# Seven block products in a decoder layer's q/k and gate/v projections, overlapped attention heads, and no spill of the residual

## The chip, the cores and the metric

The kernel runs on one core of a Trainium2 chip. A core has a matrix engine (TensorE, PE in the profile, with its weight loads as PEld), three engines for elementwise work (VectorE or DVE, ScalarE or ACT, GpSimd or POOL), a queue engine (SyncE or SP) and 16 DMA engines that move data between memory and the core's own SBUF. TensorE writes into PSUM, of which this kernel uses eight banks. The metric is the device time of one execution in microseconds.

## The reference

Two decoder layers run over one residual stream h of 256 tokens by 2048 features, all in float32. Layer 0 has one input projection that feeds two groups of heads: sliding-window attention (16 query heads in 4 groups, each group with one key and value head) and an mLSTM with 4 heads of width 256. Layer 1 has forgetting attention (FoX, 16 heads of width 128). Each mixer is followed by a SwiGLU FFN.

```python
def swa_mlstm_mixer(xn, w_in, w_out, sinks, b_i, b_f, head_gain):
    proj = xn @ w_in
    q_s, k_s, v_s, q_m, k_m, v_m, o_m, i_m, f_m = split_cols(proj, EVEN_SIZES)
    attn = sliding_window_attention(q_s, k_s, v_s, sinks)        # heads reshaped
    i_pre = softcap(i_m + b_i)
    f_pre = softcap(f_m + b_f)
    h = mlstm_chunkwise(q_m, k_m, v_m, i_pre, f_pre)              # heads reshaped
    h = rms_norm(h, head_gain)
    mem = sigmoid(o_m) * h
    return concatenate([attn, mem]) @ w_out

def forgetting_attention_mixer(xn, w_in, b_f, w_out):
    q, k, v, f = split_cols(xn @ w_in, FOX_SIZES)
    c = cumsum(log_sigmoid(f + b_f))
    s = q @ k.T * scale + c[:, None] - c[None, :]                 # causal, softmax
    return (softmax(s) @ v) @ w_out

for layer in range(2):
    h = h + mixer(rms_norm(h, norm_mix[layer]))
    h = h + (silu(xn @ w_gate) * (xn @ w_up)) @ w_down            # xn = rms_norm(h, norm_ffn)
return rms_norm(h, norm_final)
```

## The kernel before

**How a product is made.** Every weight block of two k-tiles by 512 columns (512 KB) is loaded by SP into a raw tile, and split into a rounded part hi (ScalarE, L166) and a rest lo (VectorE, L167), both in the matrix engine's fast float32 form. The activations are split in the same way (xh, xl for the normed input; mh, ml for a mixer's or FFN's inner values). A product of a 128x128 activation block with a 128x512 weight block is then three matmuls (hi·xh, lo·xh, hi·xl), accumulated in one PSUM bank. There are two 128-row blocks of tokens, so an output of 512 columns takes two banks and 16 k-tiles x 2 row blocks x 3 = 96 matmuls: this is `project` with `gemm` (L182 to L199).

**Pairs with seven block products.** `pair_group` (L423) works two outputs of 512 columns at once, over the same activations. Its `order` lists eight positions of two k-tiles. A position marked 0 is plain: eight block products. A position marked 1 is mixed: sums and differences of the activation blocks (`sums_of`, L238, tile sx) and of the weight blocks (L462 to L465, VectorE) are formed, split again, and multiplied in seven block products, four of which go into banks of their own (prods). When the group ends, `prods` are combined (L490 to L494) and the four plain banks are added. The plain banks come from one PSUM pool and the prods from the other: pa (tag acc) and pm have four banks each, and a group whose plain banks lie in pa takes all of pm for its prods. The FFN and layer 1's q with k are made this way already; layer 0's mixer is not.

**Layer 0's mixer.** The order in the program is: k and v of SWA while x is transposed; the first half of SWA's q and its groups 0 and 1, the second half and groups 2 and 3 (`swa`, `attention` with its inner `rest`), each group brought to its end before the next begins; the last part of the output gate with the mLSTM gates' columns (264 columns) and the gate arithmetic (pu, pn, pb); the rest of the gate (512 and 256 columns); mLSTM's q, its k, the first half of v, heads 0 and 1, the second half of v, heads 2 and 3 (`mlstm`, L831); then the output projection `out_proj` (L400). The latter takes 12 of 16 k-tiles for two outputs first and the last four after them, so that head 3 (k-tiles 14 and 15) is wanted last. h is x all the while.

**Layer 1's mixer.** The last 256 columns of v with the forget gate (272 columns), the fourth v block (256), three sums of x, then for each of four head groups: q with k as a pair group, the previous attention's `rest`, the decay tile, that group's v, and the attention's first half. The split halves of mixed weights (hw) lie in the space of h, which was therefore written to memory (spill) at the end of layer 0 and is read back before layer 1's FFN.

**What sets the order.** Each engine runs its own instruction list in order. The lists are made ahead of time by a planner that goes through the program with a cost model: an instruction is placed when the planner thinks that its operands and its tile's slot are there, and later work that is ready is placed ahead of earlier work that is not. Tiles of one tag share a fixed number of slots (bufs): 6 for hi and lo, 4 for raw, 2 for hv, one for c. Some work has due positions (`later`, `todo`, run at a numbered step of a gemm or a group by `run_due`).

Of the kernel before, what the change touches and what calls it, by code (L numbers as in the profile page):

```python
# [43 lines left out]
MIX = ((0, 0), (1, 1), (0, 2), (1, 3), (0, 4), (1, 5), (0, 6), (0, 7))  # L44
NX = 3
# [14 lines left out]
def trunk(  # L60
# [43 lines left out]
    gn = [gp.tile([2 * KT, P], F32, name=f"gn{i}") for i in range(2)]  # L104
    nc.scalar.dma_start(gn[0], norm_mix.rearrange("l (k p) -> (l k) p", p=P))

    def load_raw(w, k0, c0, n, pool=wr, bufs=4):
        raw = pool.tile([P, CK, NB], F32, tag="raw", name="raw", bufs=bufs)
# [7 lines left out]
    spill = dp.tile([P, NT, D], F32, name="spill")  # L116
# [21 lines left out]
    nc.gpsimd.dma_start(gn[1], norm_ffn.rearrange("l (k p) -> (l k) p", p=P))  # L138
# [8 lines left out]
    gT = cp.tile([P, 4 * KT], F32, name="gT")  # L147

    def gain_columns(i):
        pg = pm.tile([P, NB], F32, tag="pm", name="pg")  # L150
        nc.tensor.transpose(pg[:, 0 : 2 * KT], gn[i], ident[0 : 2 * KT, 0 : 2 * KT])
        nc.vector.tensor_copy(gT[:, 2 * i * KT : 2 * (i + 1) * KT], pg[:, 0 : 2 * KT])
# [85 lines left out]
    def sums_of(pool, sh, sl, copies, full=None, tags=("tmp", "tmp")):  # L238
        if full is None:
            full = pool.tile([P, 2, NT, P], F32, tag=tags[0], name="full")  # L240
            copies(full.rearrange("p i t q -> p i (t q)"))
        s = pool.tile([P, 4, P], F32, tag=tags[1], name="s4")
# [6 lines left out]
    def split_scaled(idx, n, extra=None, joined=None):  # L249
        for half in range(2):  # L250
# [8 lines left out]
            for i in range(2):  # L259
                k = 4 * n + 2 * half + i  # L260
                src = pt[:, i, :, :].rearrange("p t q -> p (t q)")
                g = gT[:, idx * KT + k : idx * KT + k + 1]
                nc.scalar.mul(xh[:, k, :], src, g)
                nc.vector.scalar_tensor_tensor(
                    out=xl[:, k, :], in0=src, scalar=g, in1=xh[:, k, :].bitcast(F32), op0=ALU.mult, op1=ALU.subtract
                )
# [42 lines left out]

    def add_out(acc, n):  # L310
# [11 lines left out]
    def attention(sp, q_of, k_of, v_of, dv, scale, bias0, bias1, k_tile, sinks=None, negc=None, s_bufs=2):  # L322
        s = sp.tile([P, 4, 3 * P], F32, tag="s", name="s", bufs=s_bufs)
        for b, cols, bias in ((0, P, bias0), (1, S, bias1)):
# [3 lines left out]
            for half in range(2):  # L328
# [7 lines left out]
                    op1=ALU.add,  # L336
                )
# [61 lines left out]

    def out_proj(w, idx, key, extra):  # L400
# [22 lines left out]
    def pair_group(fp, par, lhs, sums, mats, order, todo=(), halves=None):  # L423
# [4 lines left out]
        t0, t1 = slice(0, P), slice(P, 2 * P)  # L428
        for pos, (kind, pair) in enumerate(order):
            k0 = 2 * pair  # L430
            if not kind:
# [18 lines left out]
            ra, rb = (load_raw(w, k0, c0, NB, fp, W_RAWS if halves else RAWS) for w, c0 in mats)  # L450
# [38 lines left out]
        c = fp.tile([P, 4, NB], F32, tag="c", name="c", bufs=1)  # L489
        nc.scalar.copy(c[:, 0, :], prods[0])  # L490
        nc.vector.tensor_tensor(out=c[:, 2, :], in0=prods[3], in1=c[:, 0, :], op=ALU.add)
        nc.vector.tensor_tensor(out=c[:, 1, :], in0=prods[2], in1=c[:, 2, :], op=ALU.add)
        nc.vector.tensor_tensor(out=c[:, 3, :], in0=prods[1], in1=c[:, 1, :], op=ALU.add)
        nc.vector.tensor_tensor(out=c[:, 2, :], in0=prods[1], in1=c[:, 2, :], op=ALU.add)  # L494
        return plain, c

    def ffn(layer, fp, sx, sd, key, todo, idx_next=None, key_next=None, finish=None):
# [6 lines left out]
        for g0, g1 in zip(PARTS, PARTS[1:]):  # L504
# [69 lines left out]
            def close(acc, n):  # L574
# [4 lines left out]
                else:  # L579
# [6 lines left out]
                    nc.gpsimd.dma_start(spill[:, :, n * NB : (n + 1) * NB], h[:, :, n * NB : (n + 1) * NB])  # L586
# [43 lines left out]
    with tc.tile_pool(name="ev", bufs=1) as ev:  # L630
        dist = ev.tile([P, S], F32, name="dist")
# [12 lines left out]
        gain = ev.tile([P, ML_H * VD], F32, name="gain")  # L644
        nc.gpsimd.dma_start(gain, mlstm_head_gain[0].partition_broadcast(P))

        def natural(sp, acc, n, name, scale=r):
# [442 lines left out]
```

## Time and profile before

| what | value |
|---|---|
| median of 3 runs (lowest, highest) | 2106.33 us (2106.03, 2108.21) |
| profiled execution | 2108.73 us |
| its span, first to last instruction | 2107.0 us |
| granted TensorE clock, mean | 0.998 |
| instructions | 26956 |
| DMA moved, mean rate | 430.92 MB, 205 GB/s |
| read from memory, written | 406.57 MB, 4.21 MB |

The profiled execution is a run of its own; its time is not among the three. Times in the rows are microseconds from the start of the span. A row of a group of instructions has busy time, the mean duration of one in nanoseconds, and the idle time of the engine just before them with what ended it. In rows of the timeline the idle time and its cause stand in brackets at the end. The row of busy time over the span in 40 slices shows how even the load is:

```profile
PE   8999999999999999999999999999999999999998
DVE  6675558999999999999887768679999999999994
ACT  6565458765577655767667665588655667556763
```

The first six slices (up to about 310 us) are layer 0's mixer, slices 20 to 26 (about 1040 to 1370 us) layer 1's; the others are FFNs and output projections.

### The profile page before, as it was taken

To read this page: it belongs to the slowest core of one execution; us is meant where nothing else is said; L and a number is where in the kernel's file an instruction comes from. 1 tells how busy PE (TensorE), PEld (TensorE's weight loads), DVE (VectorE), ACT (ScalarE), POOL (GpSimd) and SP (SyncE) were. 2 spreads that over 40 slices of the span, in tenths; PEclk is the share of its full clock that TensorE was granted. 3 is DMA by queue.
4 is the path that set the end of the run, shared out by engine and by line. 5 is a ranking of instruction groups with operands and counts; after the bars stand their busy time and mean duration, and the time that the engine had idled before them with its cause. 6 is when DMAs were issued, how large, how long until landed. Compare 5 with 4: busy or idle time off the path is not lost.

```text
span 2107.0 us, 26956 instructions
## 1 busy us (share of the span) xinstructions
PE 2089.5 (99%) x9583; PEld 1733.8 (82%) x9583; DVE 1783.3 (85%) x2322; ACT 1328.5 (63%) x1681; POOL 49.1 (2%) x75
## 2 busy tenths in 40 slices
PE   8999999999999999999999999999999999999998
PEld 7888888888888888888888888888888888888886
DVE  6675558999999999999887768679999999999994
ACT  6565458765577655767667665588655667556763
POOL 2010000000000000000000000000000000000000
PEclk9999999999999999999999999999999999999999
DMA  8454548666567666667587676486756567666663
GB/s 266 149 157 150 170 146 276 229 203 215 192 198 231 230 193 210 212 218 218 178 256 206 192 218 210 140 250 213 233 188 224 196 205 238 212 198 203 224 199 136
DMA packets 290855, 430.92 MB, mean 205 GB/s; under 512 B 89024, under 2 KB 97312, under 8 KB 290464
## 3 DMA queue, kind: packets, MB, share of 16 engines
q1 hardware_dynamic: 288896, 421.27, 63.2%
q0 software_dynamic: 1776, 7.92, 1.1%
q8 instruction: 75, 1.23, 0.2%
q14 instruction: 60, 0.49, 0.1%
q10 hardware_dynamic: 48, 0.02, 0.0%
HBM read 406.57 MB, written 4.21 MB: 195 GB/s over the span
## 4 chain that ended last, share of the span: by engine, by line
PE 98%; DMA 1%; ACT 0%; issue 0%; DVE 0%; POOLq 0%; POOL 0%; DVEq 0%; ACTq 0%
PE acc L416 19%; PE acc L418 19%; PE acc L417 19%; PE acc L197 8%; PE acc L199 8%; PE acc L198 8%; PE prod L418 5%; PE prod L416 5%; PE prod L417 5%; PE p L327 1%; PE po L386 1%; DMA raw<-in_w_in_odd_dram 1%; PE ptm L319 0%; PE pp L378 0%; PE po L387 0%
## 5 line engine op out<-in xcount | busy, mean ns | idle before, releaser
L166 ACT CAST hi<-raw 128x1024 fp32r<-128x1024 f32 (+2 forms) x669 | 679.9, 1031 | 517.4 <-PE acc L418 271.9
L167 DVE TENSOR_TENSOR lo<-raw,hi 128x1024 fp32r<-128x1024 f32 (+2 forms) x669 | 791.6, 1198 | 202.9 <-ACT hi L166 200.1
L417 PE MATMUL acc<-lo,xh 128*128 128x512 f32 x1118 | 435.1, 389 | 0.0
L416 PE MATMUL acc<-hi,xh 128*128 128x512 f32 x1118 | 434.9, 390 | 0.0
L418 PE MATMUL acc<-hi,xl 128*128 128x512 f32 x1118 | 431.8, 389 | 0.0
L418 PEld LDWEIGHTS acc<-hi,xl 128*128 128x128 f32 x1118 | 209.9, 188 | 44.2
L417 PEld LDWEIGHTS acc<-lo,xh 128*128 128x128 f32 x1118 | 209.8, 188 | 44.0
L416 PEld LDWEIGHTS acc<-hi,xh 128*128 128x128 f32 x1118 | 209.8, 188 | 43.9 <-ACT hi L166 0.2
L197 PE MATMUL acc<-hi,xh 128*128 128x512 f32 (+3 forms) x480 | 174.7, 370 | 2.6 <-ACT hi L166 2.6
L198 PE MATMUL acc<-lo,xh 128*128 128x512 f32 (+3 forms) x480 | 175.9, 368 | 0.0
L199 PE MATMUL acc<-hi,xl 128*128 128x512 f32 (+3 forms) x480 | 174.4, 367 | 0.0
L417 PE MATMUL acc<-lo,mh 128*128 128x512 f32 x437 | 169.7, 389 | 0.0
L418 PE MATMUL acc<-hi,ml 128*128 128x512 f32 x437 | 168.4, 389 | 0.0
L416 PE MATMUL acc<-hi,mh 128*128 128x512 f32 x437 | 167.9, 389 | 0.0
L197 PE MATMUL acc<-hi,mh 128*128 128x512 f32 x320 | 125.4, 393 | 1.2 <-ACT mh L307 1.2
L307 ACT CAST hi<-raw 128x512 fp32r<-128x512 f32 x107 | 66.4, 621 | 94.9 <-PE acc L418 81.4
L198 PE MATMUL acc<-lo,mh 128*128 128x512 f32 x320 | 125.4, 392 | 0.0
L199 PE MATMUL acc<-hi,ml 128*128 128x512 f32 x320 | 123.4, 391 | 0.0
L308 DVE TENSOR_TENSOR lt<-t,ht 128x1024 fp32r<-128x1024 f32 x95 | 115.8, 1219 | 5.2 <-ACT ht L307 5.2
L307 ACT CAST ht<-t 128x1024 fp32r<-128x1024 f32 x95 | 99.9, 1051 | 31.7 <-PE prod L418 25.5
L307 ACT CAST ht<-raw 128x1024 fp32r<-128x1024 f32 x95 | 99.6, 1049 | 29.6 <-PE acc L418 15.0
L308 DVE TENSOR_TENSOR lt<-raw,ht 128x1024 fp32r<-128x1024 f32 x95 | 115.7, 1218 | 1.8 <-ACT ht L307 1.8
(335 smaller groups left out, 3375.3 us busy)
## 6 DMA issues: line engine op xcount, KB each, us to landing
raw<-in_w_gate_dram SPq DMA_DIRECT2D x176, 512.0 KB, 4.5
raw<-in_w_up_dram SPq DMA_DIRECT2D x176, 512.0 KB, 4.7
raw<-in_w_down_dram SPq DMA_DIRECT2D x176, 512.0 KB, 5.2
raw<-in_w_in_odd_dram SPq DMA_DIRECT2D x88, 512.0 KB, 4.7
raw<-in_w_in_even_dram SPq DMA_DIRECT2D x64, 512.0 KB, 4.2
raw<-in_w_out_even_dram SPq DMA_DIRECT2D x32, 512.0 KB, 3.7
raw<-in_w_out_odd_dram SPq DMA_DIRECT2D x32, 512.0 KB, 4.7
raw<-in_w_in_odd_dram SPq DMA_DIRECT2D x8, 272.0 KB, 2.9
```

Of the source, the lines that this page charges most:

```text
L166: latest[0] = nc.scalar.copy(hi[:, :, 0:n], raw[:, :, 0:n])
L167: nc.vector.tensor_tensor(out=lo[:, :, 0:n], in0=raw[:, :, 0:n], in1=hi[:, :, 0:n].bitcast(F32), op=ALU.subtract)
L197: nc.tensor.matmul(o, ah[:, ts], hi, start=(k == 0), stop=False)
L198: nc.tensor.matmul(o, ah[:, ts], lo, start=False, stop=False)
L199: nc.tensor.matmul(o, al[:, ts], hi, start=False, stop=(k == k_all - 1))
L307: nc.scalar.copy(dst_h, src)
L308: nc.vector.tensor_tensor(out=dst_l, in0=src, in1=dst_h.bitcast(F32), op=ALU.subtract)
L327: nc.tensor.matmul(pq[j % 2][:, j // 2, :], q_of(j, b), k_of(j)[:, 0:cols], start=True, stop=True)
L386: nc.tensor.matmul(po, v_of(j, 0), t0[:, j, :], start=True, stop=False)
L416: nc.tensor.matmul(o, ah, hi, start=start, stop=False)
L417: nc.tensor.matmul(o, ah, lo, start=False, stop=False)
L418: nc.tensor.matmul(o, al, hi, start=False, stop=stop)
```

## The change

1. **Layer 0's mLSTM q with k** become one pair group (order MIXQ), and **the gate's first 512 columns with v's first 512** another (MIXV), with three mixed positions each. The raw weight blocks of mixed positions take the space of SWA tiles that are done (tags kd, qn and twice alibi), the split halves the upper half of mh and ml, which the mixer fills only later (`spare_halves`), and the sums of x the space of h.
2. **Order of layer 0:** SWA's first half; gate tail and gate arithmetic, with the decay matrix dt_; SWA's second half; three sums of x; gate columns 512 to 767; v's second half; q with k; gate with v; then all four heads.
3. **Overlap:** the two SWA groups of a half run their first halves one after the other and then their two `rest`; a head's transposes and split (`finish`) come after the next head's first half. `ce` gets two slots instead of one tile for all heads.
4. **h is loaded again from x** by four POOL DMAs after the mixer; the spill at the end of layer 0 and the read back in layer 1 are removed, and layer 1 uses `spare_halves` as well.
5. **Layer 1:** v's first two blocks are a pair group after the first q/k group, the other two follow one group ahead of their use; the fourth is no longer at the start. The first q/k group has two mixed positions (MIX0), and the sums of x have due positions in it. The previous attention's `rest` runs inside a group ahead of its last position (`inner`), after the prods are combined.
6. The head gain goes into the split of the mLSTM output as a column factor (`split_gained`), and no longer into the gate on POOL. For the first three FoX groups the causal mask of the first block is put on the scores by POOL instead of on a copy of the decay tile.

```diff
+MIX0 = ((0, 0), (0, 1), (0, 2), (1, 3), (0, 4), (1, 5), (0, 6), (0, 7))
+MIXQ = ((0, 0), (0, 2), (1, 1), (0, 4), (1, 3), (0, 6), (1, 5), (0, 7))
+MIXV = ((0, 0), (0, 2), (0, 4), (1, 1), (0, 6), (1, 3), (1, 5), (0, 7))
...
+    def split_gained(dst_h, dst_l, src, col):
+        g = gT[:, col : col + 1]
+        nc.scalar.mul(dst_h, src, g)
+        nc.vector.scalar_tensor_tensor(
+            out=dst_l, in0=src, scalar=g, in1=dst_h.bitcast(F32), op0=ALU.mult, op1=ALU.subtract
+        )
...
+            if causal and b == 0:
+                o = s[:, :, 0:P]
+                nc.gpsimd.affine_select(
+                    out=o, in_=o, pattern=[[0, 4], [-1, P]], compare_op=ALU.is_ge, fill=NEG, base=0, channel_multiplier=1
                 )
...
+    def spare_halves():
+        return [
+            tuple(
+                m[:, 8 + 4 * a : 12 + 4 * a, :].rearrange("p k s -> p (k s)").rearrange("p (c n) -> p c n", c=2)
+                for m in (mh, ml)
+            )
+            for a in range(2)
+        ]
...
+            if inner is not None and pos == len(order) - 1:
+                c = combine(prods)
+                inner()
...
-                    nc.gpsimd.dma_start(spill[:, :, n * NB : (n + 1) * NB], h[:, :, n * NB : (n + 1) * NB])
...
+        hs_ = cp.tile([P, 2, len(mixed_of(MIXQ)), 4, P], F32R, tag="h", name="hs")
+        sx = [hs_[:, i, :, :, :] for i in range(2)]
...
+            for rest in [swa(2 * half + i, qn) for i in range(2)]:
+                rest()
...
+        swa_half(1, ev.tile([P, NT, NB], F32, tag="qn", name="qn"))
+        for j, pair in enumerate(mixed_of(MIXQ)):
+            sums_of(sw, sx[0][:, j, :, :], sx[1][:, j, :, :], whole(xh, xl, pair), tags=("qt", "qt"), bufs=2)
...
+        gate_out(project(wi, OFF_OM + NB, 256), NB, 256)
+        values(1, project(wi, OFF_VM + NB, NB))
...
+            def pair_even(c0, c1, order):
+                plain, c = pair_group(mp, 0, x_of, sums_m, [(wi, c0), (wi, c1)], order, halves=halves, raws=raws, inner=lambda: None)
+                for m in range(2):
+                    for t in range(NT):
+                        o = c[:, 2 * m + t, :]
+                        nc.vector.tensor_tensor(out=o, in0=plain[m][t], in1=o, op=ALU.add)
+                return c
...
-            qm = natural(mp, project(wi, OFF_QM, NB), NB, "qm", scale=rq)
+            c = pair_even(OFF_QM, OFF_KM, MIXQ)
...
-            km = natural(mp, project(wi, OFF_KM, NB), NB, "km")
...
+            c = pair_even(OFF_OM, OFF_VM, MIXV)
+            gate_out([c[:, t, :] for t in range(NT)], 0, NB)
+            values(0, [c[:, 2 + t, :] for t in range(NT)])
...
+            ends = []
+            for hh in range(ML_H):
+                ends.append(mlstm(hh))
+                if hh:
+                    ends.pop(0)()
+            ends.pop(0)()
+
+    h = cp.tile([P, NT, D], F32, tag="h", name="h")
+    for n in range(4):
+        nc.gpsimd.dma_start(h[:, :, n * NB : (n + 1) * NB], xv[:, :, n * NB : (n + 1) * NB])
...
-        v3 = nat1(project(wi1, c_v + 3 * NB, VT), VT, "v3")
...
-        for j, pair in enumerate(mixed_of(MIX)):
-            sums_of(od, sx[0][:, j, :, :], sx[1][:, j, :, :], whole(xh, xl, pair), tags=("t0", "t1"))
+        todo = [(p, sums_of_x(j, pair)) for p, j, pair in [(1, 1, 3), (3, 2, 5), (6, 0, 1)]]
...
-        hw = cp.tile([P, 2, 2, 2, NB], F32R, tag="h", name="hw")
-        halves = [(hw[:, a, 0, :, :], hw[:, a, 1, :, :]) for a in range(2)]
+        halves = spare_halves()
...
+            c = pair_nat(i * NB, FOX_H * FD + i * NB, todo if i == 0 else (), MIX if i else MIX0, rest)
...
+            if i == 0:
+                todo, later[:] = list(later), []
+                c = pair_nat(c_v, c_v + NB, todo)
...
+            elif i < 3:
+                n = NB if i == 1 else VT
+                vs.append(nat1(project(wi1, c_v + (i + 1) * NB, n), n, "vn", bufs=2))
...
-    h = cp.tile([P, NT, D], F32, tag="h", name="h2")
-    nc.gpsimd.dma_start(h, spill)
```

More of the change, by code (lines that the diff above doesn't have):

```diff
@@ L488, in pair_group @@
             three(plain[0][1], xb[:, t1], lb[:, t1], ht[3], lt[3], False, False)
[L489 to L494, printed above, removed]
+        if inner is None:
+            c = combine(prods)
         return plain, c
@@ new lines, in trunk @@
+        for g in range(2):
+            pb = pm.tile([P, 2, NT, P], F32, tag="pm", name="pb")
+            for i in range(2):
+                nc.tensor.matmul(
+                    pb[:, i, :, :].rearrange("p c q -> p (c q)"), sel[:, 2 * g + i, :], mt, start=True, stop=True
+                )
+            nc.vector.tensor_tensor(
+                out=dt_[:, 2 * g : 2 * g + 2, :, :].rearrange("p h c q -> p (h c) q"),
+                in0=pb.rearrange("p h c q -> p (h c) q"),
+                in1=future[:, None, :].broadcast_to([P, 4, P]),
+                op=ALU.add,
+            )
@@ L885, in trunk @@
     with tc.tile_pool(name="od", bufs=1) as od:
+        sx = [od.tile([P, NX, 4, P], F32R, name=f"sx{i}") for i in range(2)]
         def nat1(acc, n, name, bufs=1):
```

278 lines of the change are left out of this document (145 added, 133 removed).

## The prediction

> **What bounds the kernel now.** I read the page first: its busy table and the chain that ended last.
>
> ```profile
> PE 2089.5 (99%) x9583; PEld 1733.8 (82%) x9583; DVE 1783.3 (85%) x2322; ACT 1328.5 (63%) x1681; POOL 49.1 (2%) x75
> PE 98%; DMA 1%; ACT 0%; issue 0%; DVE 0%; POOLq 0%; POOL 0%; DVEq 0%; ACTq 0%
> ```
>
> The chain is TensorE for 98% of the span, so time is won by taking matmuls away or by closing a hole between them, and by nothing else. A matmul's price must not be read from its mean duration. The next view is busy time by stage (columns: stretch, its length, then per engine busy microseconds with the number of instructions, granted clock, DMA share, GB/s), beside one group row and four neighbouring instructions.
>
> ```profile
> L417 PE MATMUL acc<-lo,xh 128*128 128x512 f32 x1118 | 435.1, 389 | 0.0
> 60.01 0.39 PE L197 MATMUL acc<-hi,xh 128*128 128x512 f32 x1
> 60.23 0.39 PE L198 MATMUL acc<-lo,xh 128*128 128x512 f32 x1
> 1400.00:1900.00 500.00, 500.00 (x2211) 414.05 (x2210) 472.37 (x587) 323.23 (x361) 0.72 (x1) 1.00 0.66 212
> 30.00:300.00 270.00, 268.82 (x1389) 222.26 (x1388) 163.44 (x259) 136.87 (x237) 20.30 (x27) 0.99 0.53 166
> ```
>
> A matmul lasts 389 ns but the next starts 0.22 us later: 500 us hold 2211 of them, 226.1 ns each. That is the price of one. The last row is layer 0's mixer: TensorE busy for 268.8 of 270 us, while VectorE has 61%. In the FFN stretch above it VectorE is busy 94.5% and TensorE still has no hole.
>
> **Step 1, fewer matmuls.** A pair position worked plainly has 2 k-tiles x 2 row blocks x 2 matrices x 3 matmuls = 24; with seven block products it has 21. Layer 0 turns q with k, and half the gate with half of v, into two groups with three such positions each: 18 matmuls less. Layer 1 turns the first two v blocks into one such group: 9 less. Layer 1's first q/k group loses one of its three (MIX0): 3 more. Net 24 x 226.1 ns = -5.4 us. Nothing hides this, since TensorE is the chain.
>
> **Step 2, layer 1's opening hole.** Moved away: the projection of the last v block, the three sums of x (from before the first group into it), and the spill of h.
>
> ```profile
> 1043.43 0.29 PE L198 MATMUL acc<-lo,xh 128*128 128x272 f32 x1
> 1043.55 0.41 PE L199 MATMUL acc<-hi,xl 128*128 128x272 f32 x2
> 1045.74 0.50 PE L197 MATMUL acc<-hi,xh 128*128 128x256 f32 x2 [1.77 <-ACT hi L166]
> 1045.07 0.62 ACT L166 CAST hi<-raw 128x512 fp32r<-128x512 f32 x1 [3.92 <-DMA raw<-in_w_in_odd_dram]
> 1035.00:1040.00 5.00, 5.00 (x44) 5.00 (x43) 4.76 (x14) 3.97 (x11) 0.80 (x2) 1.00 0.96 300
> 1040.00:1045.00 5.00, 3.96 (x32) 3.74 (x30) 2.81 (x6) 1.15 (x3) 1.00 (x1) 1.00 1.04 381
> spill<-h POOLq DMA_DIRECT2D x4, 512.0 KB, 6.6
> h<-spill POOLq DMA_DIRECT2D x1, 2048.0 KB, 9.9
> ```
>
> TensorE stood 1.77 us for a cast, the cast 3.92 us for a weight block, and the DMA engines were full (share 0.96 and 1.04). The four 512 KB spills follow the last down projection's output blocks, two of them into this stretch (1.05 MB); at 381 GB/s that is 2.8 us of DMA time, more than the hole. Without them it should close. What is late next is the same queue of weights, now 512 KB blocks for the first group. Bounds 0 and -1.8; I take -1.5, nearer the row. The read back of 2 MB at the end of layer 1 goes; in its place four 512 KB loads of x go through POOL's queue once the sums' space is free, that is at the end of the gate/v group. They have to land before the first output block is added to h, about 32 us later; the old read took 9.9 us. Cost nothing; without that cover at most those 9.9 us.
>
> **Step 3, SWA groups two at a time.** The rows show the old order: TensorE's first transposes of a group come only when the group before reaches its last products.
>
> ```profile
> 62.50 0.27 PE L319 MATMUL ptm<-ident,qn 128*128 128x128 f32 x1
> 87.06 0.65 PE L386 MATMUL po<-t,vs 128*64 128x256 f32 x2
> 87.64 0.33 PE L319 MATMUL ptm<-ident,qn 128*128 128x128 f32 x1
> 116.92 0.33 PE L319 MATMUL ptm<-ident,qn 128*128 128x128 f32 x1
> 144.05 0.33 PE L319 MATMUL ptm<-ident,qn 128*128 128x128 f32 x1
> 174.68 0.38 PE L732 MATMUL pu<-ident,gates 128*4 128x128 f32 x2
> 184.56 0.33 PE L319 MATMUL ptm<-ident,qm 128*128 128x128 f32 x1
> 62.50:184.50 122.00, 122.00 (x719) 100.55 (x717) 80.77 (x145) 70.77 (x143) 10.81 (x15) 1.00 0.51 154
> ```
>
> A group takes 25 to 30 us, the gate arithmetic 10 more, 122 together, one after another, and TensorE is full all the same (122.00 of 122.00) because projections fill in. So overlapping them wins nothing by itself. It is needed, because a group with block products takes all four pm banks, which SWA also uses: the q/k group's first mixed position cannot start until SWA is through. Work that TensorE has until then, from 62.5: gate tail and second gate part, 96 narrow matmuls each at 0.12 us (start to start of 1043.43 and 1043.55 above), 24; second half of q, and second half of v, 96 x 0.226 each, 43; two plain positions of the group, 48 x 0.226 = 11; SWA's and the gates' own products, about 30 (122 less the projections that lie in that stretch: two narrow ones, three of 22, the first matmuls of k, some 92). Sum 108. Two at a time, at 30 to 35 us per couple, the chain needs 70 to 80: no hole. One at a time it needs 122: 14 us of hole. I take 0.
>
> **Step 4, the four mLSTM heads at the end.** Now heads 0 and 1 run beside the second v projection; after the change all four follow the gate/v group.
>
> ```profile
> 230.31 0.59 PE L833 MATMUL pc<-ve,kw 128*128 128x257 f32 x2
> 247.51 0.60 PE L865 MATMUL ptv<-ident,hv 128*128 128x128 f32 x4
> 247.94 0.38 PE L833 MATMUL pc<-ve,kw 128*128 128x257 f32 x1
> 263.32 0.60 PE L865 MATMUL ptv<-ident,hv 128*128 128x128 f32 x4
> 263.76 0.60 PE L833 MATMUL pc<-ve,kw 128*128 128x257 f32 x2
> 278.22 0.38 PE L833 MATMUL pc<-ve,kw 128*128 128x257 f32 x1
> 294.74 0.60 PE L865 MATMUL ptv<-ident,hv 128*128 128x128 f32 x4
> 296.52 0.50 PE L197 MATMUL acc<-hi,mh 128*128 128x512 f32 x1 [1.18 <-ACT mh L307]
> 297.15 0.68 DVE L308 TENSOR_TENSOR ml<-ptv,mh 128x512 fp32r<-128x512 f32 x1
> ```
>
> Each head starts 0.4 us after the transposes of the one before, every time: the order of the pm banks in the program holds it back, not its data. From the first pc to the last ml are 67.5 us for four. Until head 3 is needed the output projection has 28 k-steps of 6 matmuls, 168 x 0.226 = 38 us, and the heads' own products add 7 (from 263.32 to 264.87 and two more): 45 us. The new order (head 1's front ahead of head 0's transposes, two hv buffers) lets two heads run abreast: about 3 us for the last adds and the v scale, then two rounds of 15.8 to 19 us and 3 us for transposes and split, 38 to 44 us. That just fits, so I leave the old hole of 1.2 us as it is: 0. Bounds -1.2, and +24 if heads still go singly (3 + 67.5 - 45.3 - 1.2).
>
> **Step 5, VectorE in the new groups.** What a mixed position costs is seen in layer 1.
>
> ```profile
> L167 DVE TENSOR_TENSOR lo<-raw,hi 128x1024 fp32r<-128x1024 f32 x99 | 119.4, 1225 | 52.4 <-ACT hi L166 52.1
> L308 DVE TENSOR_TENSOR hw<-raw,hw 128x1024 fp32r<-128x1024 f32 x24 | 28.7, 1218 | 1.4 <-ACT hw L307 1.4
> L462 DVE TENSOR_TENSOR raw<-raw 128x512 f32<-128x512 f32 x12 | 8.3, 689 | 1.3 <-DMA raw<-in_w_in_odd_dram 1.2
> 1061.00:1127.00 66.00, 66.00 (x295) 54.25 (x293) 53.74 (x62) 46.19 (x53) 5.17 (x4) 1.00 0.81 232
> ```
>
> One takes 1.2 + 2 x 1.2 + 5 x 0.69 = 7.1 us of VectorE for 21 x 0.226 = 4.7 us of TensorE. A group has three, ten plain casts of 1.2, and eight adds of 0.69: 39 us against 41.4 of TensorE, 94%. That is the FFN's load, which runs without holes, and layer 1's groups do so too (66.00 of 66.00). But the gate/v group also carries the q/k head preparation: five copies and two products of 0.69, eight scalings of a quarter of that width (estimate 0.2 each), 6.4 us, against about 4 us of TensorE. 45.5 of 45.4: over the FFN's 94.5%. At that rate it takes 48.1 us, 3 us more. The sums of x (each two operations of 0.69 and four of a quarter width, estimate 2.5 us, three of them) can fall into the q/k group, and in layer 1 into the first group: at worst 5 us more. Bounds 0 and +8; I take +1.0, since work can be pulled ahead by the six cast buffers. ScalarE has only the casts of it, 46.19 of 66 in the same stretch.
>
> **Moves that cost nothing:** head gain folded into the split (POOL multiplies go, and VectorE's scaled split takes the place of the plain one; POOL is busy 2%); the causal mask moved from the decay tile to the scores (POOL, between VectorE's scores and their maximum, a group ahead of its use; without that cover, some 1 us per group); the previous attention's rest put ahead of a group's last position (same products, other place); layer 1's split halves in spare mh/ml instead of h's space.
>
> **Sum.** -5.4 - 1.5 + 0 + 0 + 1.0 = -5.9 us. The profiled execution took 2108.7 (span 2107.0, 1.7 around it), so its like would be 2102.8; the median shown is 2106.3, 2.4 lower, and the same step from it gives 2100.4.
>
> **Rivals.** *VectorE gives it back:* step 5 at its upper end and step 2's hole refilled: 2106.3 - 5.4 + 3 to 8 = 2103.9 to 2108.9. For it: the full VectorE of the second group. Against: layer 1.
>
> *Heads or SWA do not overlap:* slower. The place is the output projection of layer 0, waiting for mh of heads 2 and 3; the price at worst 2106.3 - 6.9 + 24 = 2123. It decides when four heads take more than 50 us (45.3 - 3 + 1.2 + 6.9) and costs over 0.2% from 54 us, 13.6 per head. For it: the singly run heads above at 15.8 us, and VectorE shared with casts. Against: 0.4 us between heads shows order, which the change alters. SWA singly would add 14 by the same rule.
>
> *The clock drops:* the transposes of q, k and scaled q now come in one clump.
>
> ```profile
> 182.67 1.97 PE L774 MATMUL pb<-mt,sel 4*128 4x256 f32 x8
> 185.09 0.78 PE L197 MATMUL acc<-hi,xh 128*128 128x512 f32 x1
> 188.22 0.43 PE L198 MATMUL acc<-lo,xh 128*128 128x512 f32 x1
> 180.00:186.00 6.00, 6.00 (x31) 4.84 (x30) 3.99 (x13) 1.97 (x6) 0.00 (x0) 0.91 0.60 178
> ```
>
> After small products and transposes the granted clock fell (0.91 in these 6 us) without any idle time, and eight matmuls from 185.09 to 188.49 took 0.43 instead of 0.23: 1.6 us. Two more dips: 2100.4 + 3.2 = 2103.6. The Trainium skill, "TensorE: Matmul & The Clock Gate", Part 4, says that transposes do not count as busy for the gate; by that rule a longer clump makes a dip likelier. The trace agrees with it in this one place; the 1.2 and 1.8 us holes above left the clock at 1.00.
>
> **How the numbers follow.** A measurement of this kernel tells about 0.2%, 4.2 us, from no change. Forecast (2097 to 2102.1, around 2100.4): 0.60. VectorE gives it back: 0.18. Clock: 0.06. Both of these end within 0.2%. No overlap: 0.16, slower. Hence faster 0.60, same 0.24, slower 0.16. All holes closed gives 2106.3 - 5.4 - 1.8 - 1.2 = 2097.9, less some scatter: low 2096.5. The upper end takes in the VectorE rival and the lighter part of the last: 2110.
>
> **What would show it.** Step 1: 24 matmuls fewer at 226 ns pitch. Step 2: no idle time before the first group's casts in layer 1, and no spill row. Step 3: TensorE full until the q/k group's first product. Step 4: pc of head 1 well ahead of head 0's ptv, and no wait of acc for mh; a wait there beyond 7 us proves me wrong. Step 5: casts of lo late, TensorE waiting for VectorE in the gate/v group.

## The result, and the profile after

The changed kernel took 2112.57 us (median of 7 runs, 2111.78 to 2116.16); the kernel before, measured beside it, 2108.55 us (7 runs, 2106.03 to 2109.91). The ratio is 1.0022 with a 95% interval of 1.0012 to 1.0031: slightly slower, where 2100.4 us was forecast. The profiled execution took 2112.44 us with a span of 2110.7 us; that of before has a span of 2107.0, so 3.7 us have to be found.

The page of the changed kernel, busy table and chain:

```profile
PE 2094.3 (99%) x9559; PEld 1728.7 (82%) x9559; DVE 1832.3 (87%) x2416; ACT 1349.0 (64%) x1709; POOL 41.9 (2%) x68
PE 98%; ACT 1%; issue 0%; DVE 0%; DMA 0%; DVEq 0%; POOLq 0%; POOL 0%; ACTq 0%
```

TensorE is still the chain. It has 24 instructions fewer (9583 before), and yet it was busy 4.8 us longer (2089.5 before). Which stage did that is seen in the windows view, cut where the stages change: layer 0's mixer with its output projection, the first FFN, layer 1's mixer with its output projection, the second FFN. First the kernel before:

```profile
30.00:345.60 315.60, 314.42 (x1590) 260.02 (x1589) 196.45 (x306) 173.80 (x290) 20.30 (x27) 0.99 0.56 176
345.60:1032.30 686.70, 686.70 (x3039) 568.56 (x3038) 647.12 (x807) 447.97 (x507) 2.13 (x3) 1.00 0.66 209
1032.30:1410.40 378.10, 376.33 (x1818) 316.21 (x1816) 287.46 (x393) 245.58 (x352) 15.17 (x17) 1.00 0.70 213
1410.40:2107.00 696.60, 687.90 (x3039) 569.29 (x3037) 634.06 (x789) 438.13 (x491) 2.43 (x4) 1.00 0.63 205
```

Then the changed kernel:

```profile
30.00:339.30 309.30, 307.51 (x1565) 254.63 (x1564) 231.53 (x378) 189.22 (x312) 14.03 (x21) 0.99 0.58 185
339.30:1032.60 693.30, 693.30 (x3039) 569.27 (x3038) 648.52 (x809) 449.55 (x508) 0.69 (x1) 1.00 0.65 206
1032.60:1407.90 375.30, 375.28 (x1811) 315.05 (x1810) 300.76 (x414) 250.57 (x359) 12.87 (x14) 1.00 0.68 206
1407.90:2110.70 702.80, 694.13 (x3039) 569.97 (x3038) 634.04 (x788) 437.36 (x489) 2.42 (x4) 1.00 0.64 203
```

The two mixers, which were changed, became 6.3 and 2.8 us shorter. The two FFNs, whose code was not changed (only the writes of h to memory at the end of the first are gone), have the same 3039 matmuls, no new hole (the 8.7 us without TensorE in the last stretch are there before and after) and a clock of 1.00, and they grew by 6.6 and 6.2 us. The pitch, which is the time from the start of one matmul to the start of the next, says the same; this is the stretch that gave 2211 matmuls before:

```profile
1400.00:1900.00 500.00, 500.00 (x2189) 410.41 (x2188) 468.60 (x582) 319.39 (x356) 0.71 (x1) 1.00 0.66 210
```

500 us by 2189 is 228.4 ns from one matmul to the next, where it was 226.1. That is no wait of any kind: each matmul itself comes a little later after the one before.

### The profile page after: what moved, and what is told of

It reads as the page before. It is cut to its first block, busy times and chain, and to the rows that moved or that the text cites. A ratio compares the mean times of both kernels' runs of the same rounds, so it can differ in the third digit from the quotient of the medians.

```text
span 2110.7 us, 27042 instructions
## 1 busy us (share of the span) xinstructions
PE 2094.3 (99%) x9559; PEld 1728.7 (82%) x9559; DVE 1832.3 (87%) x2416; ACT 1349.0 (64%) x1709; POOL 41.9 (2%) x68
## 4 chain that ended last, share of the span: by engine, by line
PE 98%; ACT 1%; issue 0%; DVE 0%; DMA 0%; DVEq 0%; POOLq 0%; POOL 0%; ACTq 0%
PE acc L442 21%; PE acc L443 21%; PE acc L444 21%; PE acc L206 6%; PE acc L207 6%; PE acc L208 6%; PE prod L442 5%; PE prod L444 5%; PE prod L443 5%; PE p L339 1%; PE po L403 1%; PE pp L395 0%; PE ptm L331 0%; PE pt L265 0%; PE po L404 0%
## 5 line engine op out<-in xcount | busy, mean ns | idle before, releaser
L175 ACT CAST hi<-raw 128x1024 fp32r<-128x1024 f32 (+3 forms) x655 | 665.9, 1030 | 472.2 <-PE acc L444 293.0
L176 DVE TENSOR_TENSOR lo<-raw,hi 128x1024 fp32r<-128x1024 f32 (+3 forms) x655 | 775.5, 1199 | 154.1 <-ACT hi L175 151.5
L443 PE MATMUL acc<-lo,xh 128*128 128x512 f32 x1254 | 491.2, 392 | 0.0
L442 PE MATMUL acc<-hi,xh 128*128 128x512 f32 x1254 | 488.9, 392 | 0.0
L444 PE MATMUL acc<-hi,xl 128*128 128x512 f32 x1254 | 487.4, 391 | 0.0
L443 PEld LDWEIGHTS acc<-lo,xh 128*128 128x128 f32 x1254 | 235.7, 188 | 51.1 <-issue 0.6
L444 PEld LDWEIGHTS acc<-hi,xl 128*128 128x128 f32 x1254 | 235.8, 188 | 50.4
L206 PE MATMUL acc<-hi,xh 128*128 128x512 f32 (+3 forms) x288 | 100.3, 352 | 0.8 <-ACT hi L175 0.8
L207 PE MATMUL acc<-lo,xh 128*128 128x512 f32 (+3 forms) x288 | 100.8, 351 | 0.0
L208 PE MATMUL acc<-hi,xl 128*128 128x512 f32 (+3 forms) x288 | 99.0, 348 | 0.0
```

The source lines that it names most:

```text
L175: latest[0] = nc.scalar.copy(hi[:, :, 0:n], raw[:, :, 0:n])
L176: nc.vector.tensor_tensor(out=lo[:, :, 0:n], in0=raw[:, :, 0:n], in1=hi[:, :, 0:n].bitcast(F32), op=ALU.subtract)
L206: nc.tensor.matmul(o, ah[:, ts], hi, start=(k == 0), stop=False)
L207: nc.tensor.matmul(o, ah[:, ts], lo, start=False, stop=False)
L208: nc.tensor.matmul(o, al[:, ts], hi, start=False, stop=(k == k_all - 1))
L442: nc.tensor.matmul(o, ah, hi, start=start, stop=False)
```

## The experiments

**What differs in an FFN whose code is the same.** Its place in SBUF. The column tile gT has 72 columns instead of 64 (the head gain's eight), 32 bytes more per partition, and every tile allocated behind it moved up by 32 bytes, the FFN pool (fp) with its sums of x (sx), raw weights, t4, ht, lt and sd among them. The split inputs (xh, xl, mh, ml) and weights (hi, lo) lie ahead of gT and did not move. A padding tile of `FILL` = 24 columns, which nothing uses, stands between. Start addresses in the built kernels, modulo 256 bytes:

```
tiles                         before   changed   changed, FILL = 16
xh, xl, mh, ml, hi, lo           128       128       128
sx, raw, t4, ht, lt, sd (FFN)    128       160       128
sx of layer 1                      0       160       128
space of h                       160       160       160
```

### The padding taken down, and put up

```diff
-FILL = 24
+FILL = 16      # e1_after_fill16: changed kernel, pool at before's address
+FILL = 32      # e2_before_fill32: kernel before, pool 32 bytes higher
+FILL = 32      # e3_after_fill32: changed kernel, pool 64 bytes above before's
```

> The changed kernel with the unused padding tile (FILL) cut from 24 to 16 columns, so that the FFN pool lies at the addresses it had before the change; nothing else differs. Placement theory (the 12.8 us that both unchanged FFN stretches grew, 686.7 to 693.3 and 696.6 to 702.8, come from the 32 bytes by which the longer gain tile gT pushed that pool): the stretches return to 686.7 and 696.6, the time falls by some 12.8 us to 9 us below the kernel before, ratio 0.9957. Rival (the changed mixers leave something behind that slows the FFN, clock or DMA or order): 2112 us, ratio 1.002, stretches of 693 and 703.

> The kernel before with the padding tile at 32 columns in place of 24, which moves the FFN pool by 32 bytes and changes nothing else. Placement theory: the FFN stretches grow to 693.3 and 702.8, the time by 12.8 us, ratio 1.006; layer 1's pool is moved too and may add a few us. Rival: no change, ratio 1.000.

> The changed kernel with the padding tile at 32 columns: the FFN pool lies 64 bytes further on than in the kernel before, at a multiple of 64 bytes but not of 128. If the period is 64 bytes: as with 16 columns, ratio 0.9957, FFN stretches 686.7 and 696.6. If the period is 128 bytes or the address itself counts: slower than that by 6 us or more. Rival that placement does not matter: ratio 1.002.

Measured, each against the kernel before (2108.83 us): e1 2098.43 us, ratio 0.9952 (0.9937 to 0.9966); e2 2121.07 us, ratio 1.0056 (1.0041 to 1.0071); e3 2110.16 us, ratio 1.0008 (0.9999 to 1.0017). The windows view of e1, the same four stages:

```profile
30.00:338.50 308.50, 306.67 (x1569) 253.35 (x1568) 231.57 (x379) 188.84 (x311) 13.44 (x21) 1.00 0.60 185
338.50:1025.10 686.60, 686.60 (x3038) 568.54 (x3037) 648.60 (x810) 450.16 (x509) 0.69 (x1) 1.00 0.67 208
1025.10:1398.60 373.50, 373.35 (x1812) 314.74 (x1811) 300.48 (x415) 250.89 (x359) 13.13 (x14) 1.00 0.69 207
1398.60:2095.20 696.60, 687.90 (x3039) 569.29 (x3037) 633.73 (x788) 437.45 (x489) 2.43 (x4) 1.00 0.65 205
```

and of e2, its two FFN stretches:

```profile
345.50:1038.70 693.20, 693.20 (x3039) 568.52 (x3038) 647.79 (x807) 447.94 (x507) 2.14 (x3) 1.00 0.66 207
1416.40:2119.20 702.80, 694.14 (x3039) 569.32 (x3038) 633.76 (x788) 437.15 (x489) 2.43 (x4) 1.00 0.64 204
```

Eight columns of an unused tile carry the loss in the FFNs and turn the sign of the result. With the pool where it was, the FFNs take 686.6 and 696.6 us again, and the change is worth 10.4 us; with the pool 32 bytes up, the kernel before has the changed kernel's FFNs. Between e1 and the changed kernel the spans differ by 15.5 us: 6.7 and 6.2 in the FFNs, 1.8 in layer 1's stretch (375.3 against 373.5), whose sx moved as well, and 0.8 in layer 0's, where the clock of the changed kernel's profiled execution dipped once (granted 0.99 in its row) and e1's did not. The medians differ by 14.1. e3 shows that 64 bytes off is no cure: its FFN stretches take 692.2 and 701.5 us.

### Which tile, and how far: first attempts

```diff
-FILL = 24
+FILL = 8                  # e5_pool_128_lower: FFN pool 128 bytes below before's
+es = sm.tile(..., bufs=1) # (also one slot less for es, rq moved into another pool)
+pad(fp, ...)              # i_*: as e5, with pads of 32 and 96 bytes between tiles of the pool
```

> The changed kernel with the FFN pool 128 bytes below where it lay in the kernel before (8 columns of padding; rq in another pool; one slot for es in place of two). A period of 128 bytes (64 bytes more were slow, 692.2 and 701.5): FFN stretches 686.7 and 696.6, time as with 16 columns of padding, some 2098 us. If the address itself counts, or a larger period: stretches of 690 or more in the first FFN, time 2104 us or more.

> As the run with the pool 128 bytes lower, and of the FFN pool only the four raw tiles, into which the weights of mixed positions are loaded, moved 32 bytes off (32 bytes of padding ahead of them, 96 behind). If transfers into misplaced tiles disturb TensorE, which is busy in aligned tiles as well: most of the 6.6 us by which the first FFN stretch grew. If only TensorE's own reads of misplaced tiles are slow: 0, since it reads no raw tile.

> The same, with only t4, ht and lt moved by 32 bytes: the sums of weight blocks and their split halves, written by VectorE and ScalarE and streamed by TensorE. Own reads: ht and lt are streamed by 12 of the 21 matmuls of a mixed position, so about half of the 6.6 us or more. Transfers: 0.

> The same, with only c and the two tmp tiles moved by 32 bytes: results on their way from VectorE and ScalarE, targets of the transposing transfers; TensorE reads none of them in the first FFN stretch but for few transposes. Own reads: 0. Traffic of the other engines: part of the 6.6 us, 1 to 3.

e5 took 2112.94 us, ratio 1.002 (1.0009 to 1.0032): 128 bytes off is as slow as 32. The three others had been written in the belief that 128 bytes down would be fast again, so their expectations do not fit what they are: runs on a slow base. They took 2111.36, 2113.68 and 2113.42 us, in one run each. Their first FFN stretches still say something (windows view of e5, i_raw_moved, i_ht_moved and i_c_moved, in this order, one row each):

```profile
339.40:1032.90 693.50, 693.50 (x3040) 569.41 (x3038) 648.06 (x809) 448.84 (x508) 0.69 (x1) 1.00 0.65 205
```
```profile
339.90:1031.80 691.90, 691.90 (x3040) 568.97 (x3038) 648.65 (x809) 449.49 (x508) 0.69 (x1) 1.00 0.65 206
```
```profile
338.50:1032.70 694.20, 694.20 (x3038) 568.93 (x3037) 648.20 (x809) 448.85 (x508) 0.69 (x1) 1.00 0.65 205
```
```profile
342.40:1034.30 691.90, 691.90 (x3040) 569.34 (x3038) 648.05 (x809) 449.23 (x508) 0.69 (x1) 1.00 0.65 206
```

In i_raw_moved and i_c_moved t4, ht, lt and sd are back at the addresses they have in the kernel before and only sx is 128 bytes off throughout; raw and c stand differently in the two, and the time is the same. So raw and c, which TensorE doesn't read (but for a few transposes), look harmless, and sx looks guilty. i_ht_moved, whose operands stand at three different places (sx and sd at 0, ht and lt at 32, the others at 128), is the slowest of the four.

### One tile alone, and all but that tile

```diff
+pad(fp, "pa_", 8); sx = ...; pad(fp, "pb_", 24)   # i_sx_alone_moved, on e5's base: only sx off, by 96 bytes
+sx = ...; fp.tile([P, 8], ...)                    # i_rest_moved, FILL = 16: all but sx off, by 32 bytes
```

> The FFN's sx (the sums of x, its stationary operand at the mixed positions) alone stands 96 bytes below the address it has in the kernel before; everything behind it (raw, t4, ht, lt, c, tmp, box, sd) is where before has it. Rests on the three runs that moved other tiles: there the first FFN stretch took 691.9 us when sx was 128 bytes low and the tiles behind it were at before's addresses. If the position of sx alone carries it: first FFN stretch 690.5 to 692.5 us, second 700.5 to 702.5. If the tiles behind carry it: 686.6 and 696.6, as in the kernel before.

> The changed kernel with the FFN pool at before's address, so that sx stands where before has it, and a pad of 32 bytes behind sx, so that all the pool's other tiles (sd, raw, t4, ht, lt, tmp, c, box) stand 32 bytes higher, as they do in the changed kernel. If sx carries most of the loss: first FFN stretch 686.6 to 688.5 us (the down projection's sd, t4, ht and lt can leave up to 1.9), second 696.6 to 698.5. If the other tiles carry it: 691 to 693.3 and 701 to 702.8.

They took 2113.61 and 2115.31 us, in one run each; the first FFN stretch of each:

```profile
342.10:1034.00 691.90, 691.90 (x3040) 568.91 (x3038) 648.57 (x810) 449.90 (x508) 0.69 (x1) 1.00 0.66 206
```
```profile
342.40:1036.10 693.70, 693.70 (x3038) 568.91 (x3037) 648.75 (x809) 449.81 (x508) 0.69 (x1) 1.00 0.65 205
```

Both are slow: sx alone costs 5.2 us, all the others without sx 7.0, both together (the changed kernel) 6.6. No single tile is guilty, and the costs don't add up: with the others 32 bytes off, it doesn't help to leave sx at its good place (693.7 us, against 693.3 with sx moved along). That speaks for the distance between tiles. The trace of i_sx_alone_moved, where sx is the only tile off, allows a closer look: its 512-column matmuls of the first FFN, grouped by where sx is the stationary operand (loaded as weights while the matmul before runs), with the mean time to the next start:

```
sx is stationary operand of               matmuls   ns to the next
neither this, the one before nor after      2449      227.3
the next one only                             80      235.3
this one (and its neighbours or not)         396      230.3 to 233.8
the one before only                           80      234.4
one before and next                            5      233.4
```

In the fast kernels it is 226.7 for all 3016. The 396 matmuls that use sx, each of them together with a streamed operand in an unmoved tile, carry 2.4 of the 5.2 us. But matmuls that read only unmoved tiles are late as well when their neighbour reads sx: these 165 carry 1.3 us, and the 2449 further away, 0.6 ns late each on average, the remaining 1.4. So the loss lies around the use of sx and not only in it: it comes where tiles that stand at different places are read in one matmul or close after one another.

### The address or the distance

```diff
+front = ...; front.tile([P, 8], ...)         # r_everything_32: 32 bytes ahead of the first tile
+mhalf, bias_g, sink, bias_f, fs, ft in front # r_distance_256: 256 bytes from behind hi, lo to ahead of xh
+ident in front                               # r_distance_512: the same with 512 bytes
```

All three have `FILL = 16`.

> The changed kernel with the FFN pool at before's address, and a pad of 32 bytes ahead of the first pool, so that every tile of the kernel but the pad stands 32 bytes higher and all mutual distances are those of the fast placement. If the distance between the FFN pool's tiles and the other operands (xh, xl, mh, ml, hi, lo) counts: FFN stretches 686.6 and 696.6 us, as in the kernel before. If the address itself counts (a multiple of 64 bytes, say): 691 to 694 and 701 to 703.

> The changed kernel with the FFN pool at before's address, and six small tiles (mhalf, bias_g, sink, bias_f, fs, ft; 256 bytes together) moved from behind the first pools to ahead of them: xh, xl, mh, ml, hi, lo stand 256 bytes higher, the FFN pool stays, so the distance is 256 bytes less. Distances off by 32 and 64 bytes one way and by 128 the other were slow (693.3, 692.2, 693.5). If the distance counts and repeats every 256 bytes: 686.6 and 696.6. If it repeats later, or only this one distance is good: 691 to 694 and 701 to 703. If only the FFN pool's own address counts: 686.6.

> The same with one tile of 512 bytes (ident) moved ahead, so that the distance is 512 bytes less. If it repeats every 256 or every 512 bytes: 686.6 and 696.6. If it repeats only after more: 691 to 694 and 701 to 703.

First FFN stretch of each, in this order:

```profile
342.30:1029.00 686.70, 686.70 (x3040) 568.60 (x3038) 647.84 (x809) 449.23 (x508) 0.69 (x1) 1.00 0.66 208
```
```profile
342.10:1028.80 686.70, 686.70 (x3040) 568.58 (x3038) 648.44 (x810) 449.86 (x509) 0.69 (x1) 1.00 0.67 208
```
```profile
339.80:1026.40 686.60, 686.60 (x3039) 568.95 (x3037) 647.70 (x809) 449.46 (x508) 0.69 (x1) 1.00 0.66 208
```

All fast (2101.40, 2100.95 and 2098.38 us in one run each; between them they differ in the mixers). Every operand shifted together by 32 bytes loses nothing: the address doesn't count. A distance changed by 256 or 512 bytes loses nothing; changes of 32, 64, 96 or 128, alone or mixed, cost about 5 to 8 us in each FFN. Other distances were not tried. So the operands that TensorE reads one after the other should start at the same place modulo 256 bytes.

### The rule used

```diff
+h = cp.tile(...)   # f_h_aligned: h ahead of the tile warm, so the space of h starts at 128 modulo 256
 warm = cp.tile(...)
+od.tile([P, 32], F32, name="pd")   # f_h_and_od_aligned: also 128 bytes behind layer 1's sx
```

> The changed kernel with the FFN pool at before's address (2098.4 us), and the tile h, whose place layer 0's sums of x (hs) take over, 32 bytes lower, so that hs too stands a multiple of 256 bytes from xh, hi and the rest. If the distance rule holds beyond the FFN: the matmuls of layer 0's mixer that read hs, 232.6 to 233.6 ns each, fall to about 226.7, and the mixer gains 0.5 to 2.5 us (some 30% of its matmuls are 4 to 12 ns long now, not all for this reason): about 2097 us. If the rule is one of the FFN pool alone: 233 ns and 2098.4 us still.

> The same, and 128 bytes of padding behind sx in layer 1's pool, so that its raw tiles and most of the others stand a multiple of 256 bytes from hi and xh too (raw was 128 off). Layer 1's attention stretch takes 275.3 to 275.8 us where nothing disturbs it, and about a sixth of its matmuls are 4 to 12 ns long. If the rule holds also for tiles that TensorE doesn't read: 274 to 275 us. If only TensorE's operands count: 275.3 to 275.8 still.

Both took `FILL = 16` along. The matmuls of layer 0 that read hs (54 prods in the trace) went from 233.1 ns in e1 to 226.7 in f_h_aligned: the rule holds outside the FFN. The time, 2097.24 us, ratio 0.995 (0.9935 to 0.9965), can't be told from e1's. Aligning layer 1's raw as well gave nothing: its 512-column matmuls have a pitch of 227.3 ns with and without (994 and 996 of them, waits left out), and 2098.83 us, ratio 0.9951 (0.9934 to 0.9968). The tiles that VectorE, ScalarE and DMA touch don't matter here, as i_raw_moved had suggested. e1 and these two beat both kernels.

### The prices of the steps

```diff
 for hh in range(ML_H):
+    mlstm(hh)()          # e4_heads_singly: FILL = 16, a head ends before the next begins
 ...
 for i in range(2):
+    swa(2 * half + i, qn)()   # swa_groups_singly: FILL = 16, the same for the SWA groups
 ...
+nc.gpsimd.dma_start(spill[...], h[...])   # spill_written_again: FILL = 16
```

> As the changed kernel with 16 columns of padding, but each mLSTM head is finished before the next begins, as in the kernel before. Step 4 of the prediction: the output projection then waits for heads 2 and 3, 24 us slower than with 16 columns alone (2123 less 12.8 of placement counted separately, about 2124). Rival (the planner's fill work covers the heads in either order): within 2 us of it.

> The changed kernel with the FFN pool at before's address (measured 2098.4 us), and the two SWA groups of a half one after the other, each finished before the next begins. My price on record for that, from the length of a group's chain under cover: +14 us. The rival, from the four mLSTM heads singly, which cost 2.9 us where the same way of pricing gave 24: 0 to +4 us, since the work between the groups covers less but the chain is also shorter when nothing else is on VectorE. By the first the first mixer (from start to the first FFN) grows from 338.5 to about 352 us, by the second to 338.5 to 342.5.

> The changed kernel with the FFN pool at before's address (measured 2098.4 us), with h written to memory again at the end of the first FFN, as the kernel before does, though nothing reads it. If the writes are what delayed layer 1's first weights: a hole of 1.5 to 1.8 us returns at the start of layer 1 (none in the changed kernel) and layer 1's mixer grows from 373.4 to about 375 us, the whole to about 2100. The rival: the hole went because the first weights are asked for elsewhere in the order; then no hole, 373.4 and 2098.4 us.

*Heads singly*: 2101.31 us, ratio 0.9965 (0.9951 to 0.9979), 2.9 us above e1 and not 24. The waits of TensorE from 240 to 300 us have one row; behind it, from the timeline, the starts of heads 1 to 3 (pc) and the last transposes of head 3 (ptv):

```profile
PE acc L206 <- ACT mh L317: 1.6, 1, 1.6
```
```profile
267.23 0.60 PE L903 MATMUL pc<-ve,kw 128*128 128x257 f32 x2
274.87 0.60 PE L903 MATMUL pc<-ve,kw 128*128 128x257 f32 x2
282.93 0.60 PE L903 MATMUL pc<-ve,kw 128*128 128x257 f32 x2
290.87 0.60 PE L938 MATMUL ptv<-ident,hv 128*128 128x128 f32 x4
```

A head takes 7.6 to 8.1 us, not the 15.8 that I had read between two heads of the kernel before.

*SWA groups singly*: 2117.57 us in one run; layer 0's stretch ends at 358.8 us instead of 338.5, 20.3 us later, where 14 were priced. The largest waits of TensorE from 100 to 262 us, and two windows of that stretch:

```profile
PE acc L442 <- ACT hi L175: 2.1, 2, 1.7
PE acc L442 <- DVE c L857: 2.1, 1, 2.1
PE acc L443 <- DVE lo L176: 1.9, 1, 1.9
PE acc L442 <- ACT hs L312: 1.7, 1, 1.7
```
```profile
160.00:180.00 20.00, 13.33 (x45) 9.05 (x44) 18.16 (x34) 9.11 (x19) 0.00 (x0) 0.75 0.50 156
205.00:220.00 15.00, 11.23 (x38) 7.95 (x37) 11.28 (x20) 5.16 (x7) 0.00 (x0) 0.77 0.64 224
```

The waits of the stretch come to 10.4 us in all. Where they are, the granted clock is at 0.75 and 0.77, and the other half of the 20.3 us goes with the slower clock. The same work in this run and, in the second row, in e1:

```profile
100.00:262.34 162.34, 151.74 (x748) 120.77 (x746) 123.68 (x202) 87.97 (x148) 3.97 (x7) 0.94 0.48 150
100.00:242.02 142.02, 142.02 (x747) 116.31 (x747) 119.78 (x188) 83.14 (x130) 1.85 (x3) 1.00 0.56 176
```

The same matmuls, but for one, kept TensorE busy 9.7 us longer, and 162.34 us at a granted clock of 0.94 instead of 1.00 are 9.7 us. About 1.7 of these lie ahead of the holes: from 100 to 160 us TensorE had none, and the clock was 0.97.

*Spill written again*: 2102.98 us in one run. Layer 1's start has its hole back (the first two of TensorE's waits from 1028 to 1060 us):

```profile
PE acc L443 <- ACT hi L176: 1.2, 1, 1.2
PE acc L444 <- DVE lo L177: 0.5, 1, 0.5
```

and in the timeline ScalarE again stands for the weight block:

```profile
1042.85 1.04 ACT L176 CAST hi<-raw 128x1024 fp32r<-128x1024 f32 x1 [4.24 <-DMA raw<-in_w_in_odd_dram]
```

The stretch from layer 1's start to its output projection took 277.5 us against 275.4 in e1: 2.1 us for writes that nobody reads. Its span is 6.0 us above e1's; 3.7 of these lie in layer 0, which the edit doesn't touch, where the granted clock was 0.98 from 100 to 246 us against 1.00 in e1.

## Why the prediction was wrong

**The step that failed is "Moves that cost nothing".** It took the head gain's place in the split for a move of work between engines and did not see that its eight columns of gT move every later tile by 32 bytes. That costs 14.1 us by the medians of e1 and the changed kernel (14.7 us in the FFNs and layer 1 by their spans), more than all the rest of the change brings. A second entry of that list failed to the good side: layer 1's split halves, moved from h's space (160 modulo 256, as the table above has it) to mh and ml (128). With the new order of layer 1's tiles its sx moved too, from 0 to 128 in e1, so that all operands stand alike there. Before, 108 prods of the halves with sx took 232.7 ns each; in e1 the 124 that there are now take 226.8. The products of hi with sx, which read no halves, fell from 236.5 to 226.6, so the gain is not that of the halves alone; the two moves were not tried apart. Over all 512-column matmuls of the stretch (waits left out) the mean fell from 229.1 to 227.3, some 1.8 us for 1000 of them. In the changed kernel sx is 32 bytes off there instead, and these prods take 232.1.

With the pool back at its place the prediction can be checked term by term. It gave -5.9; e1's span is 11.8 shorter than before's, its median 10.4, and at 2098.43 us it lies within the range given. That it does is in part luck: a good part of the gain comes from terms that the sum doesn't have.

- **Step 1, -5.4:** right. 24 matmuls fewer, and in e1 the pitch is that of before:

```profile
1400.00:1900.00 500.00, 500.00 (x2211) 414.03 (x2210) 472.25 (x588) 322.93 (x357) 0.71 (x1) 1.00 0.67 212
```

- **Step 2, -1.5:** right, with its cause: the hole of 1.77 us is gone (29.98 of 30.00 us busy at layer 1's start in the changed kernel, first row of the last fence of this section), and a hole comes back with the spill. In e1 TensorE's idle time in layer 1's stretch fell from 1.77 to 0.15 us, a gain of 1.6.
- **Step 3, 0 and 14 if singly:** the direction is right, the size was short. One hole that I did not expect came in, 1.7 us at 85 us, where TensorE's transposes wait for SWA's weights from VectorE (s). The price of 14 counted idle TensorE time (10.4 measured) but not the slower clock (9.7 measured).
- **Step 4, 0 with bounds -1.2 and +24:** the end is -1.2, since the wait for mh is gone. The +24 was mis-sized by a factor of eight: the 15.8 us between two heads of the kernel before, where a v projection runs beside them, is not the length of the chain. In e4, with all heads behind the projections, the same chain took 8. That the work on the v projection had stretched it is a reading; no run takes it apart. So the rival of heads that do not overlap, with 0.16, was a rival worth 3 us.
- **Step 5, +1.0:** too high, there was no cost. VectorE was at 94% in layer 1 from 1060 to 1100 us, at 85% from 159 to 243 us, over most of layer 0's two new pairs, and at 91% ahead of that, and TensorE has no hole in any of these; rows of the changed kernel, layer 1's start first:

```profile
1032.00:1062.00 30.00, 29.98 (x182) 26.69 (x181) 25.93 (x51) 21.69 (x37) 1.09 (x1) 1.00 0.78 255
1060.00:1100.00 40.00, 40.00 (x182) 32.84 (x181) 37.67 (x49) 26.39 (x31) 2.69 (x3) 1.00 0.67 197
112.00:159.00 47.00, 47.00 (x269) 38.91 (x267) 42.67 (x84) 35.72 (x74) 0.00 (x0) 0.96 0.54 176
159.00:242.90 83.90, 83.90 (x392) 68.57 (x392) 71.69 (x89) 43.40 (x49) 1.86 (x3) 1.00 0.54 176
```

- **The clock rival:** no further dips; one in the changed kernel's layer 0 (0.96 over 47 us in the third row above, some 1.7 us), as before, and none in e1's profiled execution, which is some 1.7 us of its 11.8. These two runs have the same instructions there, so the clump of transposes alone doesn't decide whether the clock dips.

Of e1's 11.8 us these make 5.4 + 1.6 + 1.2 - 1.7 + 1.8 (halves and sx of layer 1) + 1.7 (clock) = 10.0; hs, misplaced by 32 bytes in h's space, takes about 0.6 back (the mean of layer 0's 512-column matmuls, about 1000, waits left out, is 227.4 ns before, 228.0 in e1 and 227.4 in f_h_aligned). The last 2.4 us, in layer 0, I did not take apart; 0.9 of them are the start, which varies from run to run (the 101st matmul starts at 29.4 us before, at 28.5 in e1 and at 27.9 in the changed kernel). The loss was in none of the rivals either: all of them looked for it in the stages that the diff touches.

## What to carry to other kernels

When a tile grows or moves, list the start addresses of the matmul operands before and after, and keep the operands that alternate on TensorE at the same place modulo 256 bytes; if a stage with unchanged code changes its pitch, look there first. An edit can be judged only after this is taken out: here eight columns of padding separate 10 us faster from 4 us slower. Only this kernel's matmuls were measured, most of them 128x512; whether other shapes and types behave so is open. The time between two steps of a chain that runs under cover is no price for that chain when the cover is gone.

## What the runs showed of the hardware

- The time from one 128x512 matmul to the next depends on where its operands and its neighbours' lie in SBUF: 226.7 ns in the FFN when all start at the same place modulo 256 bytes, 228.9 on average in the changed kernel, and 230 to 235 for matmuls that read a tile out of step or stand next to one that does (sx moved alone). The Trainium skill, "TensorE: Matmul & The Clock Gate", Part 2, "Step-by-step: what each phase is for", says that TensorE has two independent read ports, and that loading the next weights doesn't take read bandwidth from the running matmul. By that one would not expect the place of the next weights to matter to the matmul before; in i_sx_alone_moved a matmul whose successor alone loads sx comes to 235.3 ns, up to 9 ns more than in step. Why is open; two reads that meet would fit it, but no run here shows the reads themselves, and the matmul behind is as late (234.4).
- Several holes close together came with a slower clock: 6.7 us of idle time between 160 and 180 us in swa_groups_singly with a granted clock of 0.75, while the single holes of 1.7 and 1.8 us of the changed kernel and the one before left it at 1.00. In that run the waits of 10.4 us came with 9.7 us more of busy time for the same matmuls. The clock also dips without a hole (0.96 with TensorE busy for 47.00 of 47 us in the changed kernel).
